# The recurrent mixer's gate and output projections as seven-product 2x2 block products

## The chip, the cores and the metric

One core of a Trainium2 chip. The metric is the device time of one launch in microseconds, and fewer is better. The engines have the profile's names: PE is TensorE (PEld its weight loads), DVE VectorE, ACT ScalarE, POOL GpSimd, SP SyncE. Every engine works through its own queue in order.

## The reference

Two encoder layers over 768 tokens (a sequence of 512 and one of 256) with 1024 channels. A layer adds half a SwiGLU FFN, a mixer, and half another FFN to x, each behind an RMS norm. The mixer of layer 0 is a bidirectional gated recurrence with eight heads of 128 channels; that of layer 1 is windowed attention. The change is in layer 0's mixer, which is, with the recurrence itself left out:

```
q, i, g, f_fw, f_bw = split(x @ w_in, 5)
o = scan_forward(q, k_f, i, f) + scan_backward(q, k_b, i, f)
o = o * rsqrt(mean(o * o, per head) + eps) * g_norm
return (o * silu(g)) @ w_o
```

Everything is float32.

## The kernel before, in words

A float32 product is made of three matmuls: each operand is split into a high part that the array takes exactly (a cast on ScalarE) and the rest (a subtraction on VectorE), and high x high, high x low and low x high are added up in PSUM. So each operand, weights too, costs one ScalarE and one VectorE pass (`split`, `plain_steps`).

Tokens are six blocks of 128 (`NBLK`), in two halves of three (`HB`); channels are eight blocks of 128. A plain projection `proj_tok` of 512 output columns takes, for each of six blocks, 8 x 3 matmuls of 128x512. The gate is two of them, `g0` and `g1`, and so is the output (`hg_o`), with 288 matmuls for the gate and 288 for the output.

A seven-product 2x2 block product cuts tokens, inner channels and output columns in halves, and forms seven products of half size in place of eight: `p1` to `p7` of sums and differences of the four weight quarters (`tok_steps`) with the four quarters of the input and their mixes `t1` to `t4` (`mix`, `FACTOR`). Each product has 3 blocks x 4 inner channel blocks x 3 matmuls = 36, all together 252. The value projection v already is one (`tok_quad`); the results are combined by adds from PSUM into its output tiles (`x11` to `x22`).

The mixer runs so: the v product, then eight scans (`hgrn_scan`), one per head, woven with the projections of later heads (`weave`, `hgrn_chunk`). A scan has seven levels; each level's scores (six 128x128 products in float32) need the queries and keys that the level before has scaled on VectorE. Into the last scan `g0` is woven in place of projections, and its result is evacuated by a Silu on ScalarE (L995) and multiplied by scan output and rstd on VectorE (L1001, 48 of 128x128). The gated blocks are then turned (transposes, L1019), scaled by the norm's gain and split (L1022, L1023), and multiplied with `w_o`. The results are added to x (L570), which has been reloaded from where it was spilled, and the next FFN's norm follows block by block (`after_block`).

Weights are loaded on SP's queue into buffers `wr`, split into buffers `w`, ahead of their use as far as free buffers allow (`ahead`, `load_next`, `done`). Which instruction stands where in an engine's queue is decided when the kernel is built: a tile layer puts the recorded instructions in order by its own estimates, except where the kernel pins them.

## Time and profile before

| what | value |
|---|---|
| median of three runs | 2788.37 us (2788.32 to 2788.64) |
| profiled execution | 2788.47 us |
| its span | 2786.7 us |
| TensorE busy | 2762.9 us, 99% |
| VectorE busy | 2191.5 us, 79% |
| ScalarE busy | 1343.8 us, 48% |
| the v product | 542 to 599 us of the span |
| scans with later heads' projections | 599 to 887 us |
| last scan with g0 | 887 to 937 us |
| g1, then output product | 937 to 975 us, 975 to 1042 us |

The profile is one execution; its span leaves out 1.8 us of the time. In a group's row the number behind the bar is the busy time of all its instructions and the mean of one in ns, then the idle time of the engine ahead of them and who ended it. A matmul's own length is modelled and overlaps the next one's; the pace of a run of them is the group's busy time over its count. In a timeline row the first number is the start in us.

### The profile page before, as it was taken

The numbers are of one execution on the slowest core, as the hardware profiler recorded it, in microseconds if no ns is written. First come the engines' busy times: TensorE is split into PE (matmuls) and PEld (weight loads), VectorE is DVE, ScalarE is ACT, GpSimd is POOL, SyncE is SP. The second block draws the span as 40 slices with busy tenths as digits, with TensorE's granted clock in tenths as the row PEclk, the third lists the DMA queues.
The fourth block names the chain that finished last, engine by engine and source line by source line (L and its number), as shares of the span: only waits on it lengthen the run. The fifth ranks groups of instructions, "written<-read, shape, count | busy, mean of one in ns | idle before, by whom it ended". The sixth has DMA issues, their size and how long they took to land.

```text
span 2786.7 us, 40646 instructions
## 1 busy us (share of the span) xinstructions
PE 2762.9 (99%) x15189; PEld 2569.4 (92%) x15189; DVE 2191.5 (79%) x3803; ACT 1343.8 (48%) x2479; POOL 376.8 (14%) x409
## 2 busy tenths in 40 slices
PE   8999999999999999999999999999999999999998
PEld 8999999989999889999999999999988889999998
DVE  8788788777887658878878887887848878778877
ACT  7344444634444435444444643444458855444443
POOL 2111111100000001211111121111002311211110
PEclk9999999999999999999999999999999999999999
DMA  6554554421111223555444365545422122655543
GB/s 176 125 131 114 123 144 128 145 69 39 39 39 31 81 81 81 144 134 124 121 114 121 84 144 127 131 114 122 129 72 76 40 66 74 148 133 129 117 114 107
DMA packets 331750, 294.53 MB, mean 106 GB/s; under 512 B 11848, under 2 KB 258080, under 8 KB 331552
## 3 DMA queue, kind: packets, MB, share of 16 engines
q1 hardware_dynamic: 294560, 213.42, 25.7%
q0 software_dynamic: 32688, 65.03, 13.9%
q10 hardware_dynamic: 4304, 13.49, 1.3%
q8 instruction: 119, 1.95, 0.3%
q14 instruction: 79, 0.65, 0.1%
HBM read 217.44 MB, written 9.44 MB: 81 GB/s over the span
## 4 chain that ended last, share of the span: by engine, by line
PE 96%; DVE 2%; ACT 1%; DMA 0%; issue 0%; DVEq 0%; ACTq 0%
PE ps L486 42%; PE ps L550 21%; PE ps L310 8%; PE ps L309 8%; PE ps L311 8%; PE ps L796 3%; PE ps L729 2%; PE ps L900 1%; PE ps L1291 1%; PE ps L876 1%; PE ps L380 1%; PE ps L1303 0%; PE ps L1253 0%; PE ps L1254 0%; PE ps L1304 0%; PE ps L1054 0%
## 5 line engine op out<-in xcount | busy, mean ns | idle before, releaser
L486 PE MATMUL ps<-big,w 128*128 128x384 f32 x6720 | 1169.3, 334 | 0.0
L486 PEld LDWEIGHTS ps<-big,w 128*128 128x128 f32 x6720 | 1165.9, 188 | 1.7 <-ACT tA L503 0.2
L205 ACT CAST w<-wr 128x512 fp32r<-128x512 f32 x600 | 416.9, 707 | 680.1 <-PE ps L486 277.7
L550 PE MATMUL ps<-w,big 128*128 128x512 f32 x2520 | 575.3, 389 | 0.0
L550 PEld LDWEIGHTS ps<-w,big 128*128 128x128 f32 x2520 | 472.8, 188 | 97.4
L206 DVE TENSOR_TENSOR w<-wr,w 128x512 fp32r<-128x512 f32 (+1 forms) x520 | 429.3, 830 | 159.4 <-ACT w L205 138.9
L572 DVE SCALAR_TENSOR_TENSOR x<-ps,x 128x512 f32<-128x512 f32 x468 | 302.5, 687 | 10.0 <-PE ps L311 9.9
L144 POOL DMA_DIRECT2D s<-wr x122 | 106.7, 877 | 1483.3 <-DMA wr<-in_ffn_w_dram 650.0
L309 PE MATMUL ps<-big,w 128*128 128x384 f32 x640 | 219.5, 345 | 1.1 <-ACT w L172 1.0
L310 PE MATMUL ps<-big,w 128*128 128x384 f32 x640 | 215.6, 337 | 0.6 <-DVE big L315 0.5
L311 PE MATMUL ps<-big,w 128*128 128x384 f32 x640 | 214.6, 335 | 0.0
L309 PE MATMUL ps<-w,big 128*128 128x512 f32 x528 | 210.9, 399 | 0.3 <-DVE big L1314 0.2
L311 PE MATMUL ps<-w,big 128*128 128x512 f32 x528 | 207.0, 392 | 0.5 <-DVE big L395 0.5
L310 PE MATMUL ps<-w,big 128*128 128x512 f32 x528 | 206.4, 391 | 0.0
L314 ACT CAST big<-tA 128x384 fp32r<-128x384 f32 x296 | 148.0, 513 | 113.8 <-DVE tA L518 36.2
L315 DVE TENSOR_TENSOR big<-tA,big 128x384 fp32r<-128x384 f32 x296 | 165.5, 570 | 6.7 <-ACT big L314 4.5
L206 POOL TENSOR_TENSOR w<-wr,w 128x512 fp32r<-128x512 f32 x80 | 133.3, 1666 | 185.8 <-ACT w L205 185.6
L144 POOL DMA_DIRECT2D wr<-wr x101 | 88.6, 877 | 422.0 <-DVE w L206 159.4
L172 ACT CAST w<-wr 128x1024 fp32r<-128x1024 f32 x84 | 88.2, 1052 | 107.3 <-PE ps L310 78.0
L173 DVE TENSOR_TENSOR w<-wr,w 128x1024 fp32r<-128x1024 f32 x84 | 102.1, 1223 | 41.7 <-ACT w L172 36.7
L212 DVE TENSOR_TENSOR wr<-wr,wr 128x512 f32<-128x512 f32 (+1 forms) x120 | 127.4, 1061 | 6.0 <-issue 5.7
L310 PEld LDWEIGHTS ps<-big,w 128*128 128x128 f32 x640 | 120.5, 188 | 1.9 <-DVE big L315 1.7
(198 smaller groups left out, 3390.8 us busy)
## 6 DMA issues: line engine op xcount, KB each, us to landing
wr<-in_ffn_w_dram SPq DMA_DIRECT2D x264, 512.0 KB, 3.9
s<-wr POOLq DMA_DIRECT2D x122, 256.0 KB, 4.8
s<-in_ffn_w_dram SPq DMA_DIRECT2D x120, 256.0 KB, 3.2
wr<-wr POOLq DMA_DIRECT2D x80, 256.0 KB, 3.9
wr<-in_hg_w_in_dram SPq DMA_DIRECT2D x36, 512.0 KB, 3.7
wr<-wr POOLq DMA_DIRECT2D x21, 512.0 KB, 4.6
spill<-x ACTq DMA_DIRECT2D x12, 512.0 KB, 4.0
x<-spill ACTq DMA_DIRECT2D x12, 512.0 KB, 3.2
```

The lines of the kernel that those rows point to most:

```text
L144: self.nc.gpsimd.dma_start(out, src, accum_op=ALU.add)
L205: nc.scalar.copy(h, src)
L206: (eng or nc.vector).tensor_sub(l, src, h.bitcast(F32))
L212: add = {"second": lambda: nc.vector.tensor_add(a11, a11, a21), "fourth": lambda: nc.vector.tensor_add(a12, a12, a11)}
L309: nc.tensor.matmul(out, a[0], b[0], start=first, stop=False)
L310: nc.tensor.matmul(out, a[0], b[1], start=False, stop=False)
L311: nc.tensor.matmul(out, a[1], b[0], start=False, stop=last)
L314: self.nc.scalar.copy(hi, src)
L315: self.nc.vector.tensor_sub(lo, src, hi.bitcast(F32))
L486: self.nc.tensor.matmul(ps, a[x], b[y], start=first and k == 0 and i == 0, stop=k == 3 and i == 2, skip_group_check=True,)
L550: nc.tensor.matmul(ps, a[x], w[y], start=name == chain and kp == 0 and q == 0, stop=kp == 1 and q == 2, skip_group_check=True,)
L572: self.nc.vector.scalar_tensor_tensor(x, ps, c, x, ALU.mult, ALU.add)
```

## The change

The gate and the output projection become seven-product block products through the same `tok_quad`, which now takes the order of products, the banks that they share (`chains`), the operands, an evacuation and a seed.

- **Operands of the gate.** They are the mixes t1 to t4 of the mixer's input, whose buffers are needed in between: `spill_factors` stores the eight tiles of 768 KB to DRAM from GpSimd's queue at the start of v, and `reload_factor` loads them on SP's, two at a time, when an earlier product of the gate has ended.
- **Last scan.** The gate's first products are woven into it, in half blocks of six matmuls. The rstd factor moves from VectorE's L1001 to ScalarE (`scaled`, 48 pieces of 128x128, 42 of them within the last scan, six at its end).
- **End of the gate.** `evac_g` adds the products up on VectorE, takes the Silu on ScalarE, and `gated` multiplies by scan output on VectorE (12 of 128x512). `turned` transposes four heads of half of the blocks at a time and evacuates them on ScalarE.
- **Output product.** `put` splits the turned tiles, `mixed` forms t1 to t4 from them on VectorE (`mix` with `early`: t3 and t2 first). The order `OUT` puts p2, p6 and p5 onto p1's banks and p7 and p4 onto p3's. Ahead of p6, p4 and p5 a ScalarE copy writes a value into the bank (`seed_o`, nine of 128x512) and the matmuls add to it.
- **Weights.** Both weight matrices are fetched in quarters, whose sums are made by accumulating DMAs on GpSimd's queue and by VectorE adds.
- x is reloaded in two halves; the masks move to another pool's buffers, the squares into spare room of kT and S.

```diff
+TCHAIN = {"p2": "p1", "p4": "p5", "p3": "p7"}
+OUT = ("p1", "p2", "p3", "p7", "p6", "p4", "p5")
...
-        sums = {"p6": (a11, a21), "p3": (a12, a11)}
+        second, fourth = (a11, a21), (a12, a11)
+        sums = {"p6": (second,), "p3": (fourth,)} if order == TOK else {}
+        behind = {"p2": (second, fourth)} if order == OUT else {}
...
+            for total, part in behind.get(name, ()):
+                for t, u in zip(total[kp], part[kp]):
+                    self.tc.keep_in_program_order(nc.vector.tensor_add(t, t, u))
...
+        inuse = lambda e: e[0] if len(e[1]) > 4 or e[0] < 4 else 0
+        while self.queue and sum(inuse(e) for e in self.loaded) + len(self.queue[0][1]) <= RAWBUFS:
...
+        if early:
+            put("t3", b22)
+            sub(b11, b11, b22)
+            put("t2", b11)
+            sub(b21, b21, b11)
+            put("t4", b21)
+            put("t1", b12)
+            return
...
+    def spill_factors(self):
+        self.kept = {}
+        for name in ("t3", "t2", "t1", "t4"):
+            for kp in range(2):
+                t = self.kept[(name, kp)] = self.dp.tile([P, 4 * H], F32, name=self.name("kept"))
+                self.nc.gpsimd.dma_start(t, self.ops[(name, kp)].bitcast(F32).rearrange("p a b c -> p (a b c)"))
+
+    def reload_factor(self, name):
+        for kp in range(2):
+            t = self.ops[(name, kp)] = self.big([P, 2, 2, H], F32R)
+            self.nc.sync.dma_start(t.bitcast(F32).rearrange("p a b c -> p (a b c)"), self.kept[(name, kp)])
...
+    def tok_quad(self, key, order, chains, ops, evac, seed=None):
+        nc = self.nc
+        banks, used = {}, []
+        for name in order:
             ws = [self.take((*key, name, kp)) for kp in range(2)]
-            chain = {"p2": "p1", "p4": "p5", "p3": "p7"}.get(name, name)
+            chain = chains.get(name, name)
             for i in range(HB):
+                fresh = (chain, i) not in banks
+                if fresh:
                     banks[(chain, i)] = self.ps()
                 ps = banks[(chain, i)]
+                if seed:
+                    seed(name, i, ps)
...
+                    if k == 1:
+                        if used and i:
+                            self.done(used.pop(0))
+                        yield name, i, 0
+                evac(name, i, ps)
+                if i == HB - 1:
+                    used += [(*key, name, kp) for kp in range(2)]
+                if i == HB - 1 or (used and not i):
+                    self.done(used.pop(0))
+                yield name, i, 1
+        for k in used:
+            self.done(k)
...
+        quad(("g",), w_in[:, 2 * D : 3 * D], TOK)
+        quad(("o",), w_o, OUT)
...
+        self.spill_factors()
+        for at in self.tok_quad(("v",), TOK, TCHAIN, self.ops, evac_v):
+            if at == ("p6", HB - 1, 1):
...
+        def evac_g(name, i, ps):
+            if name == "p1":
+                if i == 0:
+                    gq["x22"] = wide()
+                nc.scalar.activation(gq["x22"][:, i], ps, AF.Copy, scale=-1.0)
+                return
+            if name == "p2":
+                if i == 0:
+                    gq["x11"] = wide()
+                nc.scalar.activation(gq["x11"][:, i], ps, AF.Silu)
+                return
+            x22 = gq["x22"][:, i]
+            if name == "p5":
+                nc.vector.tensor_sub(x22, x22, ps)
+                if i == 0:
+                    gq["s22"] = wide()
+                nc.scalar.activation(gq["s22"][:, i], x22, AF.Silu)
+                gated(1, 1, i)
+            elif name in ("p4", "p3"):
+                q = "x21" if name == "p4" else "x12"
+                if i == 0:
+                    gq[q] = wide()
+                t = gq[q][:, i]
+                if name == "p4":
+                    nc.vector.tensor_add(t, ps, x22)
+                else:
+                    nc.vector.tensor_sub(t, ps, x22)
+                nc.scalar.activation(t, t, AF.Silu)
+                gated(int(name == "p3"), int(name == "p4"), i)
+            else:
+                nc.vector.tensor_add(x22, ps, x22)
+
+        def gated(half, part, i):
+            b = half * HB + i
+            sg = gq["s22" if half and part else f"x{part + 1}{half + 1}"][:, i]
+            u = vs[b][:, part * 512 : (part + 1) * 512]
+            nc.vector.tensor_mul(u, u, sg)
+
+        def scaled(first, last):
+            for b in range(NBLK):
+                for h in range(first, last):
+                    u = vs[b][:, h * P : (h + 1) * P]
+                    nc.scalar.activation(u, u, AF.Copy, scale=rs[:, h, b : b + 1])
+
+        uops, un = {}, {}
+
+        def turned(half, part):
+            t = un[(part, half)] = self.big([P, 2, 2, H])
+            for j in range(4):
+                h = 4 * part + j
+                pt = self.ps(H)
+                for i in range(HB):
+                    src = vs[half * HB + i][:, h * P : (h + 1) * P]
+                    nc.tensor.transpose(pt[:, i * P : (i + 1) * P], src, self.ident)
+                gn = self.cols[:, gn_row + h : gn_row + h + 1]
+                nc.scalar.activation(t[:, j // 2, j % 2, :], pt, AF.Copy, scale=gn)
+            if (part, half) != (0, 1):
+                for kp in range(2):
+                    self.put(f"b{part}{half}", kp, t[:, kp], uops)
+
+        def mixed(kp):
+            tiles = (un[(i // 2, i % 2)][:, kp] for i in range(4))
+            self.mix(*tiles, lambda name, src: self.put(name, kp, src, uops), True)
+
+        def gate():
+            need = {"p1": "t3", "p2": "t2", "p7": "t1", "p6": "t4"}
+            for at in self.tok_quad(("g",), TOK, TCHAIN, self.ops, evac_g):
+                if at[1:] == (HB - 1, 1) and at[0] in need:
+                    self.reload_factor(need[at[0]])
+                yield at
+
+        feed = itertools.chain(stream(), gate())
...
-        g0 = self.proj_tok("g0", put_g(0))
-        for _ in range(lead):
-            next(g0)
-        self.weave(scan(heads[-1]), g0, 24 - lead)
-        self.drain(g0)
-        rstds(1)
-        self.drain(self.proj_tok("g1", put_g(1)))
-        self.reload_x()
-        self.drain(self.out_proj("hg_o", 0, uT, None))
-        self.drain(self.out_proj("hg_o", 1, uT, next_row))
+            self.weave(scan(heads[h]), feed, 16 if h == 0 else 18)
+        rstds(0, HEADS - 1)
+        self.weave(scan(heads[-1]), feed, 20, also=lambda i: i < HEADS - 1 and scaled(i, i + 1))
+        rstds(HEADS - 1, HEADS)
+        scaled(HEADS - 1, HEADS)
+        for i in range(HB):
+            gated(0, 0, i)
+        for at in feed:
+            if at == ("p5", 1, 0):
+                turned(0, 0)
+            elif at == ("p4", 1, 1):
+                turned(1, 1)
+            elif at == ("p3", 1, 0):
+                turned(0, 1)
+                self.reload_x(range(HB))
+        def seed_o(name, i, ps):
+            src = {"p6": "first", "p4": "sum", "p5": "sum"}.get(name)
+            if src:
+                nc.scalar.activation(ps, oq[src][:, i], AF.Copy, scale=-1.0 if name == "p5" else 1.0)
+
+        def evac_o(name, i, ps):
+            if name == "p1":
+                if i == 0:
+                    oq["first"] = wide()
+                nc.scalar.activation(oq["first"][:, i], ps, AF.Copy, scale=-1.0)
+            elif name == "p3":
+                if i == 0:
+                    oq["third"], oq["sum"] = wide(), wide()
+                nc.scalar.copy(oq["third"][:, i], ps)
+            elif name == "p7":
+                nc.vector.tensor_sub(oq["sum"][:, i], ps, oq["third"][:, i])
+                nc.vector.tensor_add(xc(HB + i, 0), ps, xc(HB + i, 0))
+            elif name == "p6":
+                nc.vector.tensor_add(oq["sum"][:, i], ps, oq["sum"][:, i])
+            elif name == "p2":
+                nc.vector.tensor_add(xc(i, 0), ps, xc(i, 0))
+            elif name == "p4":
+                nc.vector.tensor_add(xc(i, 1), ps, xc(i, 1))
+                self.after_block(i, next_row)
+            else:
+                b = HB + i
+                nc.vector.tensor_sub(xc(b, 1), xc(b, 1), ps)
+                nc.vector.tensor_add(xc(b, 0), ps, xc(b, 0))
+                self.after_block(b, next_row)
+                if b >= 4:
+                    self.run_later()
+
+        chains = {"p2": "p1", "p6": "p1", "p5": "p1", "p7": "p3", "p4": "p3"}
+        for name, i, end in self.tok_quad(("o",), OUT, chains, uops, evac_o, seed_o):
+            if (name, i, end) == ("p1", 1, 0):
+                turned(1, 0)
+                self.reload_x(range(HB, NBLK))
+            elif (name, i, end) in (("p2", 0, 0), ("p2", 1, 1)):
+                mixed(int(i))
```

On each engine the rows ahead of the last scan and behind the mixer are the same as before, but for the eight stores.

PE, in the last scan, before: 12 of the gate's matmuls (L309, L310, L311) between two levels' scores (L796). These are the last ten of them and the scores.

```order
L311 MATMUL ps_1131_7994<-w_1112_7887,big_690_4709 128x512
L309 MATMUL ps_1131_7994<-w_1112_7887,big_690_4709 128x512
L310 MATMUL ps_1131_7994<-w_1113_7888,big_690_4709 128x512
L311 MATMUL ps_1131_7994<-w_1112_7887,big_690_4709 128x512
L309 MATMUL ps_1136_8041<-w_1056_7476,big_659_4611 128x512
L310 MATMUL ps_1136_8041<-w_1057_7477,big_659_4611 128x512
L311 MATMUL ps_1136_8041<-w_1056_7476,big_659_4611 128x512
L309 MATMUL ps_1136_8041<-w_1056_7476,big_659_4611 128x512
L310 MATMUL ps_1136_8041<-w_1057_7477,big_659_4611 128x512
L311 MATMUL ps_1136_8041<-w_1056_7476,big_659_4611 128x512
L796 MATMUL ps_1137_8049<-big_1119_7921,big_1124_7965 128x128 x4
L796 MATMUL ps_1138_8050<-big_1119_7921,big_1124_7965 128x128 x2
```

PE at the same place, now; L827 are the scores, L764 the gate's matmuls.

```order
L827 MATMUL ps_1142_8097<-big_1112_7892,big_1125_7990 128x128 x4
L827 MATMUL ps_1143_8098<-big_1112_7892,big_1125_7990 128x128 x2
L764 MATMUL ps_1132_8025<-w_1108_7871,big_690_4709 128x512 x2
L764 MATMUL ps_1132_8025<-w_1109_7872,big_690_4709 128x512
L764 MATMUL ps_1132_8025<-w_1108_7871,big_690_4709 128x512
L827 MATMUL ps_1148_8147<-big_1112_7892,big_1125_7990 128x128 x4
L827 MATMUL ps_1149_8148<-big_1112_7892,big_1125_7990 128x128 x2
L764 MATMUL ps_1150_8167<-w_1133_8039,big_1135_8045 128x512
L764 MATMUL ps_1150_8167<-w_1134_8040,big_1135_8045 128x512
L764 MATMUL ps_1150_8167<-w_1133_8039,big_1135_8045 128x512 x2
```

Between two levels' scores stand four matmuls of the gate where twelve stood.

ACT in the last scan, before: L826 copies the keys for a level's scores, L995 is the gate's Silu.

```order
L826 COPY big_1124_7965<-big_1120_7922 128x768 x2
L995 ACTIVATE tA_1134_8034<-ps_1131_7994 128x512
L826 COPY big_1124_7965<-big_1120_7922 128x768
L995 ACTIVATE tA_1139_8081<-ps_1136_8041 128x512
L826 COPY big_1124_7965<-big_1120_7922 128x768 x2
L995 ACTIVATE tA_1146_8143<-ps_1143_8103 128x512
L826 COPY big_1124_7965<-big_1120_7922 128x768
L995 ACTIVATE tA_1161_8237<-ps_1148_8150 128x512
```

ACT at the same place, now: L857 is the copy of the keys, L1078 the rescaling of scan output (x, by hrs), L323 the cast of a weight (w from wr).

```order
L323 CAST w_1144_8138<-wr_1044_7393 128x1024
L1078 ACTIVATE x_749_5109<-x_749_5109,hrs_5457 128x128
L1078 ACTIVATE x_742_5076<-x_742_5076,hrs_5457 128x128
L1078 ACTIVATE x_745_5092<-x_745_5092,hrs_5457 128x128
L1078 ACTIVATE x_748_5108<-x_748_5108,hrs_5457 128x128
L1078 ACTIVATE x_743_5077<-x_743_5077,hrs_5457 128x128
L1078 ACTIVATE x_746_5093<-x_746_5093,hrs_5457 128x128
L1078 ACTIVATE x_749_5109<-x_749_5109,hrs_5457 128x128
L1078 ACTIVATE x_742_5076<-x_742_5076,hrs_5457 128x128
L1078 ACTIVATE x_745_5092<-x_745_5092,hrs_5457 128x128
L1078 ACTIVATE x_748_5108<-x_748_5108,hrs_5457 128x128
L857 COPY big_1125_7990<-big_1113_7893 128x768
```

Ten rescalings and a weight's cast have come ahead of the copy of the keys.

DVE in the output product, before: adds into x from PSUM (L570) and two weight splits (L173).

```order
L570 TENSOR_TENSOR x_1232_8634<-ps_1242_8690,x_1232_8634 128x512
L570 TENSOR_TENSOR x_1233_8636<-ps_1243_8704,x_1233_8636 128x512
L570 TENSOR_TENSOR x_1234_8638<-ps_1244_8718,x_1234_8638 128x512
L173 TENSOR_TENSOR w_1247_8740<-wr_1218_8585,w_1246_8739 128x1024
L570 TENSOR_TENSOR x_1235_8640<-ps_1245_8732,x_1235_8640 128x512
L173 TENSOR_TENSOR w_1250_8753<-wr_1221_8597,w_1249_8752 128x1024
L570 TENSOR_TENSOR x_1230_8630<-ps_1252_8758,x_1230_8630 128x512
```

DVE in the output product, now: the mix of the turned blocks (L426, L427, L430, L432), the splits of the mixes (L324, 128x2x384) and of weights (L324, w), and the adds into x (L1147).

```order
L426 TENSOR_TENSOR big_1215_8577<-big_1244_8746,big_1215_8577 128x768
L324 TENSOR_TENSOR w_1254_8795<-wr_1171_8314,w_1253_8794 128x1024
L324 TENSOR_TENSOR big_1255_8806<-big_1215_8577,big_1255_8806 128x2x384
L430 TENSOR_TENSOR big_1202_8481<-big_1202_8481,big_1215_8577 128x768
L324 TENSOR_TENSOR w_1260_8828<-tA_1172_8316,w_1259_8827 128x512
L432 TENSOR_TENSOR big_1227_8651<-big_1227_8651,big_1202_8481 128x768
L324 TENSOR_TENSOR big_1256_8810<-big_1202_8481,big_1256_8810 128x2x384
L324 TENSOR_TENSOR w_1260_8828<-tA_1173_8317,w_1259_8827 128x512
L324 TENSOR_TENSOR big_1257_8814<-big_1227_8651,big_1257_8814 128x2x384
L324 TENSOR_TENSOR big_1258_8817<-big_1244_8746,big_1258_8817 128x2x384
L1147 TENSOR_TENSOR x_1235_8680<-ps_1243_8739,x_1235_8680 128x512
L427 TENSOR_TENSOR big_1244_8746<-big_1202_8481,big_1244_8746 128x768
```

A block of sixteen passes of 128x768, eight for each half of the inner channels, has come between the adds into x.

156 lines of the change are left out of this document (57 added, 99 removed).

## The prediction

> **What bounds the kernel now.** I read the page first: busy shares and the chain that ended last.
>
> ```profile
> span 2786.7 us, 40646 instructions
> PE 2762.9 (99%) x15189; PEld 2569.4 (92%) x15189; DVE 2191.5 (79%) x3803; ACT 1343.8 (48%) x2479; POOL 376.8 (14%) x409
> PE 96%; DVE 2%; ACT 1%; DMA 0%; issue 0%; DVEq 0%; ACTq 0%
> ```
>
> TensorE is never short of work, and the chain runs through it. So a matmul that goes is worth its whole pace, and an idle gap on TensorE costs its whole length. The profiled run took 2788.47 us, 1.8 more than its span, and 0.1 more than the median. Next the stages, in windows: the value projection v, the scans, the last scan with gate half g0, gate half g1, the output product, and the start of the FFN.
>
> ```profile
> core 0: us, PE busy (x) PEld busy (x) DVE busy (x) ACT busy (x) POOL busy (x), PEclk, DMA share, GB/s
> 542.00:599.30 57.30, 57.30 (x255) 47.45 (x255) 37.35 (x51) 23.37 (x34) 1.97 (x1) 1.00 0.26 74
> 599.30:887.00 287.70, 287.15 (x2007) 283.90 (x2006) 232.17 (x404) 127.07 (x230) 0.00 (x0) 1.00 0.14 41
> 887.00:937.50 50.50, 50.50 (x306) 44.52 (x305) 40.42 (x84) 22.70 (x40) 0.00 (x0) 1.00 0.11 34
> 937.50:975.00 37.50, 37.50 (x180) 31.34 (x179) 15.99 (x37) 14.28 (x21) 0.00 (x0) 1.00 0.31 103
> 975.00:1042.00 67.00, 66.91 (x314) 55.76 (x313) 33.66 (x52) 21.02 (x34) 1.73 (x2) 1.00 0.29 83
> 1042.00:1100.00 58.00, 58.00 (x343) 57.66 (x342) 48.94 (x69) 37.72 (x66) 10.12 (x7) 1.00 0.38 91
> ```
>
> TensorE has no gap in any of them. VectorE is busy for 80% beside the scans but for 43% and 50% in the g1 and output stages. The change fills just these two. The table of waits agrees: from 484 to 1100 us TensorE's matmuls waited twice.
>
> ```profile
> PE ps L796 <- ACT big L826: 0.5, 1, 0.5
> PE ps L310 <- DVE big L315: 0.3, 1, 0.3
> ```
>
> **What goes.** Gate and output lose 36 of 288 matmuls each: 72 of 128x512. The seven-product matmul is in the trace already, for v:
>
> ```profile
> L729 PE MATMUL ps<-w,big 128*128 128x512 f32 x252 | 57.3, 389 | 0.0
> ```
>
> 57.3/252 = 0.2274 us each (389 ns is the modelled length; they overlap), so 72 are worth **16.4 us**. The 48 transposes remain. All TensorE rows before the last scan and after the mixer are the same, so everything else is decided between 887 and 1042.
>
> **What comes: the last scan.** One level of the scan is a loop: scores on TensorE, two masked copies and the scaling of q on VectorE, the copy of k on ScalarE, scores. Its timeline:
>
> ```profile
> 916.25 1.50 PE L796 MATMUL ps<-big,big 128*128 128x128 f32 x12
> 917.34 1.07 DVE L815 COPY_PREDICATED big<-big,ps 128x512 f32<-128x512 uint8 x2 [0.48 <-PE ps L796]
> 917.83 0.84 ACT L826 COPY big<-big 128x768 f32<-128x768 f32 x1 [2.14 <-PE ps L796]
> 918.30 0.95 DVE L848 TENSOR_TENSOR big<-big,big 128x768 f32<-128x768 f32 x1
> 919.57 1.03 DVE L852 TENSOR_TENSOR big<-big,big 128x384 f32<-128x384 f32 x2
> 920.32 1.50 PE L796 MATMUL ps<-big,big 128*128 128x128 f32 x12
> ```
>
> Next scores can follow 916.25 no sooner than 919.25 (end of the q scaling), about 3.2 us with the hand-over. Between the two scores lie 12 product matmuls, so the scores themselves take 4.07 - 12 x 0.2274 = 1.34 us, and some 8 matmuls must lie between. In the new order one pair of levels has 4: 3.2 - 1.34 - 0.91 = 0.95 us of gap. At the next level there are 12 again (4.07 us), but the chain has a weight split of 1.22 (row below) ahead of the k scaling (1.03), then the k copy (0.84) among ten rescalings on ScalarE: 1.1 to the first masked copy, + 1.07 + 0.95 + 1.22 + 1.03 + 0.84 = 6.2, a gap of 2.1. The rescaling (48 head-by-block pieces, 42 of them in this scan) is priced by the nearest ScalarE row, a 128x128 copy, 8.8/42 = 0.21 each back to back; it replaces 48 VectorE pieces of 0.29:
>
> ```profile
> L906 ACT COPY x<-ps 128x128 f32<-128x128 f32 x42 | 8.8, 302 | 0.0
> L1001 DVE SCALAR_TENSOR_TENSOR tA<-x,hrs,tA 128x128 f32<-128x128 f32 x48 | 13.9, 348 | 20.2 <-ACT tA L995 20.2
> ```
>
> 42 x 0.21 = 8.8 us onto 22.7 of ScalarE work; with split casts and evacuations it has about 40 of 50 us. The other four hand-overs, an estimate from the same rows, cost 0.2 to 0.9 each, 1.75 together. Sum **4.8 us**, between 2.5 (only the counted gaps shrunk by work done early) and 8 (each rescaling 0.30).
>
> **The end of the gate.** Behind the last scan ScalarE switches function tables twice:
>
> ```profile
> 936.88 0.49 ACT L906 COPY x<-ps 128x128 f32<-128x128 f32 x2
> 937.39 1.28 ACT L984 ACT_TABLE_LOAD   x1
> 938.69 0.32 ACT L984 ACTIVATE hrs<-hss,eps 128x24 f32<-128x24 f32 x1
> 942.33 1.28 ACT L995 ACT_TABLE_LOAD   x1
> 943.62 0.60 ACT L995 ACTIVATE tA<-ps 128x512 f32<-128x512 f32 x1
> ```
>
> ```profile
> L907 DVE TENSOR_REDUCE hss<-tA 128x4 f32<-128x512 f32 x2 | 1.4, 678 | 0.0
> ```
>
> Now the first four evacuations of turned blocks queue behind both loads, the square root, six rescalings, a Silu and six copies of scan output: 2.6 + 0.3 + 1.3 + 0.6 + 1.3 + 1.0 (two squares, the second of half the width), and 1.3 of waiting for VectorE's two reductions and the reciprocal, 8.4 us. TensorE has 28 matmuls and 9 transposes (12 take 1.23 us from 1039.08 to 1040.31, quoted below), 7.3 us, until the next transpose needs the bank that the first evacuation (0.6) frees: a gap of 1.7. The two later rounds of transposes add, as an estimate, 1.4. Sum **3.1 us**, from 1.5 to 5. In the rows a load costs 1.28 and nothing more: 937.39 follows 937.37, and 938.69 follows at once. [...]
>
> **The output product.** Its operands are now made on VectorE: 8 subtractions and 8 splits of 128x768 in one block, beside weight splits and sums and three adds into x.
>
> ```profile
> L315 DVE TENSOR_TENSOR big<-big,big 128x768 fp32r<-128x768 f32 x16 | 14.6, 956 | 3.1 <-ACT big L314 3.1
> L173 DVE TENSOR_TENSOR w<-wr,w 128x1024 fp32r<-128x1024 f32 x38 | 46.3, 1223 | 22.1 <-ACT w L172 22.0
> L570 DVE TENSOR_TENSOR x<-ps,x 128x512 f32<-128x512 f32 x24 | 16.6, 690 | 26.3 <-PE ps L311 26.3
> ```
>
> From the second product's weight split until p7's weights are split VectorE has 16 x 0.91 (14.6/16) + 4 x 1.22 + 13 x 0.69 = 28.5 us, in order. TensorE has p1, p2, p3 and 12 transposes for cover, 108 x 0.2274 + 1.2 = 25.8. So p7 waits at least 2.7; the mix itself cannot start before the last turned blocks are evacuated, and p3's second split is late by about 0.8. Sum **4.1 us**, from 2.6 to 6.2. The nine seeds cost nothing: a product of the same bank ended at least a product (8.2 us) earlier, and two blocks (5.4 us) cover the last sum (0.69) and the seed (0.6, from a ScalarE 128x512 like the Silu above); without that cover 1.3 for each of the two later products.
>
> **The seam to the FFN.**
>
> ```profile
> 1039.08 1.47 PE L380 MATMUL ps<-ident_r,big 128*128 128x128 f32 x12
> 1040.31 0.60 PE L309 MATMUL ps<-big,w 128*128 128x384 f32 x2
> 1041.11 0.19 PEld L310 LDWEIGHTS ps<-big,w 128*128 128x128 f32 x1 [0.40 <-DVE big L315]
> ```
>
> Before, only a 0.4 us gap. Now the last product needs two adds per block instead of one (0.69 more) ahead of the norm, and evacuations stand behind the norms of two blocks. **1.8 us**, from 0.7 to 2.6.
>
> **Transfers.** Eight 768 KB stores in v, from GpSimd's queue ahead of the mask cast, and eight loads on SP's, one product ahead:
>
> ```profile
> POOL big L128 <- DVE w L315: 34.7, 1, 34.7
> wr<-in_hg_w_o_dram SPq DMA_DIRECT2D x8, 512.0 KB, 5.4
> x<-spill ACTq DMA_DIRECT2D x6, 512.0 KB, 3.2
> ```
>
> GpSimd idled 34.7 us before that cast, and 6.3 MB in 57.3 us add 110 GB/s to 74. A load scaled by size lands in 4.8 to 8.1 us, less than a product of 36 matmuls (8.2). The last load (t4) is queued behind output weights whose buffers VectorE frees late; I take 0, at most 4 us. The x loads in two halves are as early as before.
>
> **Sum.** 2788.5 - 16.4 + 4.8 + 3.1 + 4.1 + 1.8 = 2785.9 for a profiled run; against the median 0.1 less, **2785.8**. The lower ends give 7.3 us of gaps (2779), the upper 21.8 (2794): the forecast's own range.
>
> **Rivals.** First, the gaps close: the gaps were counted one by one, but a gap at one hand-over gives VectorE and ScalarE time that the next has to spare. The v stage speaks for it, a seven-product form with no gap at 65% VectorE. Against it, VectorE's 28.5 us against 25.8 do not go away. With about 4 us left, 2776 (2772 to 2782).
>
> Second, slower: VectorE becomes the bound from the gate's p5 to the output's p7. The p5 to p3 rows hold 24 x 0.69 + 3 x 1.22 + 6 x 0.91 = 25.7, so 54.2 us with the above, against 53.9 on TensorE (216 x 0.2274 + 48 x 0.10). Any idleness of VectorE then lengthens the stretch; the forecast's 7.2 us of gap there make its share 89%. Its busiest windows show 232.17/287.70 = 81% and 48.94/58 = 84%. At 81% the stretch takes 66.9 us, 13.0 of gap, 19.6 with scan and seam: 2791.6. At 75% 18.4 and 25.0: **2797** (2794 to 2802, the latter at 70%). It is slower by over 5.6 us from a share under 78%. For it: every split waits for a cast on a ScalarE that is itself full. Against it: in those windows VectorE mostly waited for TensorE, without need.
>
> Third, the t4 load is late by its full 4 us: 2790.
>
> **Chances.** Forecast 0.42, of which 0.12 lies below 2782.8; gaps close 0.29; VectorE bound 0.25; late load 0.04. A measurement tells 0.2% (5.6 us) from no change. Faster by more 0.12 + 0.29 = 0.41; within 0.30 + 0.04 = 0.34; slower 0.25. The range leaves out the lowest third of the closing gaps and the upper two fifths of the VectorE bound: 2774 to 2798.
>
> **What would show it.** The output stage's VectorE share over 85% until p7, with a gap of about 3 us ahead of p7's first matmul; gaps of 1 and 2 us between scan levels; gaps at the gate's last transposes ended by ScalarE; none ended by a DMA. Four gap groups under 1 us each would prove the first rival. I am wrong if gaps lie outside 887 to 1042, in v for instance, or if matmuls slow down under the added transfers.

## The result, and the profile after

The changed kernel takes 2783.04 us (median of 15 runs, 2781.01 to 2785.44) against 2788.39 us (15 runs, 2788.01 to 2788.88) in the same session: 5.3 us less, a ratio of 0.9981 with an interval of 0.9974 to 0.9988. The forecast was 2785.8, a gain of 2.6: the gain is about twice that. Besides the median the scatter has changed: 4.4 us between the ends of its runs, where the kernel before has 0.9.

The head of the page of the changed kernel; the profiled run took 2783.55 us:

```profile
span 2781.6 us, 40766 instructions
PE 2750.1 (99%) x15117; PEld 2555.3 (92%) x15117; DVE 2228.3 (80%) x3825; ACT 1387.6 (50%) x2586; POOL 393.9 (14%) x431
```

The 72 matmuls are gone from TensorE's count (15189 to 15117). The FFN starts at 1034.72 us where it started at 1040.31, and v at 542.4 instead of 541.99, so the mixer behind v's start is 6.0 us shorter. 16.4 us of matmuls went, and with them the 0.5 us wait of the kernel before, which stood in the last scan but one (0.6 counted as below); so 11.0 us came back. The table of waits from 484 to 1100 us says where (line, wait in total, times, longest):

```profile
PE ps L764 <- ACT big L1140: 2.6, 2, 2.3
PE ps L827 <- ACT big L857: 1.9, 1, 1.9
PE ps L319 <- DVE big L324: 0.7, 2, 0.4
PE ps L827 <- DVE big L879: 0.7, 1, 0.7
PE ps L764 <- DVE w L324: 0.6, 1, 0.6
PE ps L932 <- DVE big L919: 0.4, 1, 0.4
PE ps L908 <- ACT big L901: 0.2, 1, 0.2
PE ps L318 <- ACT big L323: 0.2, 1, 0.2
```

No wait is ended by a DMA, and none by a seed (L1130). L827 is the scan's scores, L764 the seven-product matmul, L318 and L319 the FFN's first. The stages in windows, now the last scan, the end of the gate, the output product until p7, its rest, with v ahead:

```profile
core 0: us, PE busy (x) PEld busy (x) DVE busy (x) ACT busy (x) POOL busy (x), PEclk, DMA share, GB/s
542.00:599.30 57.30, 57.30 (x255) 47.51 (x254) 37.49 (x51) 23.46 (x34) 4.42 (x6) 1.00 0.51 165
884.00:935.00 51.00, 47.70 (x287) 41.20 (x286) 41.42 (x77) 36.47 (x87) 2.62 (x3) 1.00 0.44 145
935.00:970.00 35.00, 35.00 (x186) 29.33 (x185) 27.76 (x40) 28.27 (x54) 3.51 (x4) 1.00 0.69 186
970.00:1000.00 30.00, 26.76 (x119) 21.23 (x118) 28.05 (x36) 19.70 (x34) 0.00 (x0) 0.98 0.37 124
1000.00:1037.00 37.00, 36.38 (x170) 30.05 (x169) 28.00 (x45) 23.04 (x40) 2.02 (x2) 0.97 0.35 91
```

v carries twice the traffic (165 GB/s, before 74) at no cost to TensorE: 57.30 of 57.30. The gaps are in the last scan (3.3 us idle) and in the output product until p7 (3.2), where VectorE is busy for 28.05 of 30 us. The clock column is new: 0.98 and 0.97, where the kernel before has 1.00 in every stage from 542 to 1100 us. In finer windows around p7:

```profile
995.00:998.00 3.00, 1.21 (x4) 0.67 (x4) 3.00 (x5) 3.00 (x6) 0.00 (x0) 1.00 0.21 59
998.00:1000.00 2.00, 1.82 (x5) 1.50 (x6) 1.94 (x4) 2.00 (x5) 0.00 (x0) 0.68 0.30 83
1000.00:1002.00 2.00, 2.00 (x6) 1.56 (x5) 0.83 (x2) 0.60 (x2) 0.00 (x0) 0.50 0.38 107
1002.00:1004.00 2.00, 2.00 (x9) 1.59 (x9) 2.00 (x4) 0.00 (x0) 0.00 (x0) 0.96 0.84 250
```

About 2 us after the gap has ended TensorE runs at half its clock for 3.4 us: 2 x 0.32 + 2 x 0.50 + 2 x 0.04 = 1.7 us lost. The table of waits cannot show this; TensorE counts as busy.

Each gap is also a little longer than its wait says. A matmul's end is modelled at 389 ns while the next starts 227 ns after it, so the wait counts 0.16 us too little. By starts, the two counted gaps of the scan, rows of the timeline:

```profile
906.06 1.17 PE L764 MATMUL ps<-w,big 128*128 128x512 f32 x4
907.94 1.58 PE L827 MATMUL ps<-big,big 128*128 128x128 f32 x12 [0.71 <-DVE big L879]
909.28 2.99 PE L764 MATMUL ps<-w,big 128*128 128x512 f32 x12
914.22 1.60 PE L827 MATMUL ps<-big,big 128*128 128x128 f32 x12 [1.95 <-ACT big L857]
```

907.94 - 906.06 - 4 x 0.2274 = 0.97 us, and 914.22 - 909.28 - 12 x 0.2274 = 2.21. The gap ahead of p7, between p3's last matmuls and p7's first:

```profile
988.17 6.19 PE L764 MATMUL ps<-w,big 128*128 128x512 f32 x26 [0.63 <-DVE w L324]
996.66 1.21 PE L764 MATMUL ps<-w,big 128*128 128x512 f32 x4 [2.30 <-ACT big L1140]
```

996.66 - 988.17 - 26 x 0.2274 = 2.58 us. The copy of p3 that this wait names (L1140) stands behind casts that waited for VectorE's mix (L430):

```profile
993.09 0.84 ACT L323 CAST big<-big 128x768 fp32r<-128x768 f32 x1 [1.94 <-DVE big L430]
996.03 0.58 ACT L1140 COPY big<-ps 128x512 f32<-128x512 f32 x1
```

### The profile page after: what moved, and what is told of

It is laid out like the page before. It is cut to its first block, busy times and chain, and to the rows that moved or that the text cites. A ratio compares the mean times of both kernels' runs of the same rounds, so it can differ in the third digit from the quotient of the medians.

```text
span 2781.6 us, 40766 instructions
## 1 busy us (share of the span) xinstructions
PE 2750.1 (99%) x15117; PEld 2555.3 (92%) x15117; DVE 2228.3 (80%) x3825; ACT 1387.6 (50%) x2586; POOL 393.9 (14%) x431
## 3 DMA queue, kind: packets, MB, share of 16 engines
q8 instruction: 119, 1.95, 0.3%
## 4 chain that ended last, share of the span: by engine, by line
PE 95%; DVE 2%; ACT 2%; DMA 0%; issue 0%; DVEq 0%; ACTq 0%
PE ps L517 42%; PE ps L581 21%; PE ps L319 6%; PE ps L318 6%; PE ps L320 6%; PE ps L764 5%; PE ps L827 3%; PE ps L932 1%; PE ps L1418 1%; PE ps L908 1%; PE ps L389 1%; PE ps L1430 0%; PE ps L1380 0%; PE ps L1381 0%; PE ps L1431 0%; PE ps L1181 0%
## 5 line engine op out<-in xcount | busy, mean ns | idle before, releaser
L581 PE MATMUL ps<-w,big 128*128 128x512 f32 x2520 | 575.6, 389 | 0.0
L581 PEld LDWEIGHTS ps<-w,big 128*128 128x128 f32 x2520 | 472.6, 188 | 97.9 <-DVE x L603 0.3
L318 PE MATMUL ps<-big,w 128*128 128x384 f32 x640 | 219.3, 345 | 2.0 <-ACT w L175 1.0
L319 PE MATMUL ps<-big,w 128*128 128x384 f32 x640 | 215.5, 337 | 0.9 <-DVE big L324 0.9
L323 ACT CAST big<-tA 128x384 fp32r<-128x384 f32 x296 | 148.0, 513 | 114.3 <-DVE tA L549 36.4
L764 PE MATMUL ps<-w,big 128*128 128x512 f32 x756 | 179.7, 395 | 3.2 <-ACT big L1140 2.6
L764 PEld LDWEIGHTS ps<-w,big 128*128 128x128 f32 x756 | 141.4, 189 | 33.5 <-ACT big L1140 3.5
L324 DVE TENSOR_TENSOR big<-tA,big 128x384 fp32r<-128x384 f32 x296 | 166.2, 572 | 6.6 <-ACT big L323 4.5
L318 PE MATMUL ps<-w,big 128*128 128x512 f32 x336 | 134.7, 401 | 0.3 <-DVE big L1441 0.2
L215 DVE TENSOR_TENSOR wr<-wr,wr 128x512 f32<-128x512 f32 (+1 forms) x120 | 122.9, 1024 | 14.2 <-issue 10.2
L320 PE MATMUL ps<-w,big 128*128 128x512 f32 x336 | 132.2, 393 | 0.5 <-DVE big L404 0.5
L319 PE MATMUL ps<-w,big 128*128 128x512 f32 x336 | 131.6, 392 | 0.0
L318 PEld LDWEIGHTS ps<-big,w 128*128 128x128 f32 x640 | 119.9, 188 | 3.2 <-ACT w L175 1.3
```

What stands on the lines that cost most here:

```text
L318: nc.tensor.matmul(out, a[0], b[0], start=first, stop=False)
L319: nc.tensor.matmul(out, a[0], b[1], start=False, stop=False)
L320: nc.tensor.matmul(out, a[1], b[0], start=False, stop=last)
L323: self.nc.scalar.copy(hi, src)
L324: self.nc.vector.tensor_sub(lo, src, hi.bitcast(F32))
L581: nc.tensor.matmul(ps, a[x], w[y], start=name == chain and kp == 0 and q == 0, stop=kp == 1 and q == 2, skip_group_check=True,)
```

## The experiments

Twelve kernels ran, each beside the kernel before on its chip (2788.4 to 2788.7 there).

| kernel | median us (range, runs) | ratio to before, interval |
|---|---|---|
| changed kernel again | 2783.02 (2781.45 to 2784.81, 11) | 0.9981 [0.9972, 0.9990] |
| gate alone changed | 2786.09 (2784.83 to 2787.23, 11) | 0.9992 [0.9983, 1.0000] |
| gap ahead of p7 filled | 2781.65 (2780.38 to 2783.15, 10) | 0.9975 [0.9966, 0.9985] |
| both large gaps filled | 2782.94 (2782.65 to 2783.40, 11) | 0.9980 [0.9971, 0.9989] |
| late splits on GpSimd | 2786.70 (2784.47 to 2788.57, 11) | 0.9994 [0.9985, 1.0003] |
| late mix | 2778.90 (2777.71 to 2779.41, 5) | 0.9965 [0.9952, 0.9977] |
| early rescaling | 2781.27 (2779.81 to 2781.84, 7) | 0.9973 [0.9963, 0.9984] |
| late mix, early rescaling | **2775.31** (2774.60 to 2776.59, 5) | 0.9953 [0.9939, 0.9967] |
| 22 pieces woven | 2782.37 (2780.66 to 2783.34, 11) | 0.9976 [0.9967, 0.9985] |
| before, gap of 1.0 us | 2790.52 (2790.30 to 2790.95, 10) | 1.0007 [0.9998, 1.0016] |
| before, gap of 2.95 us | 2793.59 (2792.67 to 2794.43, 10) | 1.0018 [1.0009, 1.0027] |
| before, gap of 5.55 us | 2797.43 (2796.75 to 2797.94, 5) | 1.0032 [1.0019, 1.0044] |

**The changed kernel again.** No edit; a second profile of the same program.

> The changed kernel once more, for a second profile and for the comparison on the same chip. If the scatter of its times (4.4 us in 15 runs, 0.9 before) comes from spells in which the granted clock halves after a gap on TensorE, each spell of 3.4 us costs 1.7 us: the times should differ by multiples of about 1.7 us, the slower ones with the lower mean clock, and this profile should show as many spells as its time lies above 2781. If the scatter comes from transfers, the clock is the same in all and gaps are ended by DMAs. Median 2783.0, range 2781 to 2786.

The median repeats. This profile (2784.48 us) has two half-clock spells, the one at p7 and one behind the scan's 2 us gap, which the first profile (2783.55 us) lacks:

```profile
912.00:914.00 2.00, 0.04 (x2) 0.02 (x1) 2.00 (x6) 2.00 (x7) 0.00 (x0) 1.00 0.00 0
914.00:916.00 2.00, 2.00 (x10) 2.00 (x11) 2.00 (x5) 2.00 (x6) 0.00 (x0) 0.53 0.00 0
916.00:918.00 2.00, 2.00 (x9) 1.72 (x9) 2.00 (x5) 1.61 (x6) 0.00 (x0) 0.62 0.00 0
```

2 x 0.47 + 2 x 0.38 = 1.7 us again. So the same gap brings a spell in one run and none in another: a source of scatter. The times do not stand in steps of 1.7 us, as was expected, and with one spell more this profile is only 0.9 us slower than the first; so the spells are not the whole scatter.

**Gate alone changed.** The output projection stays as before (turned blocks written as split halves by ScalarE and VectorE, two plain halves behind them).

```diff
-        quad(("o",), w_o, OUT)
+        self.plan_out("hg_o", w_o)
...
-                nc.scalar.activation(t[:, j // 2, j % 2, :], pt, AF.Copy, scale=gn)
...
+                nc.scalar.activation(hi, pt, AF.Copy, scale=gn)
+                nc.vector.scalar_tensor_tensor(lo, pt, gn, hi.bitcast(F32), ALU.mult, ALU.subtract)
...
+        self.drain(self.out_proj("hg_o", 0, uT, None))
+        self.drain(self.out_proj("hg_o", 1, uT, next_row))
```

> Only the gate is a seven-product block product; the output projection is the plain one of 288 matmuls with its operands split as before. Theory: the gate alone takes 36 matmuls away (8.2 us) and brings the last scan's gaps (3.3 us by the waits, about 4 with the pipeline's refill) and in some runs a half-clock spell there (1.7 us): 2783 to 2785.5, so that the output's half brings little or nothing (8.2 less 4 of gaps, 1.7 of spell and the seam). Rival: the gate pays for all, the output stage loses as much as it saves or more: 2781 to 2783. Second rival: both halves gain alike: 2785.5 to 2786.

2786.09 us: above the range of the first theory and 0.1 above that of the second rival, by which both halves gain alike. The gate's half brings 2.3 us of its 8.2, the output's half 3.05. The scan's waits are the same 1.9 + 0.7 + 0.4 + 0.2, and its profile has a spell at 914 to 918.

**Gap ahead of p7 filled.** Fifteen matmuls whose result nothing reads, on operands that are ready, keep TensorE at work in the gap (`NFILL` is 15).

```diff
+            if name == "p7":
+                idle = self.ps()
+                h = uops[("b11", 1)][:, 1, 0, :]
+                for j in range(NFILL):
+                    self.tc.keep_in_program_order(
+                        nc.tensor.matmul(idle[:, :H], h[:, :P], h, start=j == 0, stop=j == NFILL - 1)
+                    )
```

> Fifteen matmuls of 128x384 into a bank that nobody reads (2.6 us) stand ahead of the output's p7, where TensorE waited 2.6 us. Theory: the wait ahead of p7 ends when it ended, so the work costs nothing, but TensorE is never idle long enough for its clock to fall: the half-clock spell behind p7's wait is gone, median 2781.3 (1.7 us less than the changed kernel), and the scatter shrinks. Rival: the clock falls for another reason (added transfers, or the mere count of small gaps): the spell stays, and the time is the same or up to 2.6 us longer.

1.4 us less than the changed kernel, though TensorE does more. The clock at p7 is 1.00 throughout:

```profile
995.00:998.00 3.00, 3.00 (x18) 2.92 (x17) 3.00 (x4) 2.87 (x6) 0.00 (x0) 1.00 0.00 0
```

What follows is no earlier for it: the next wait for a copy of p3, 0.3 us around 998 us, is there as in the first profile of the changed kernel. So the spell went with the idle time and not with the lateness, and the median is 1.4 us lower. The gap in the scan still brings one (from 914.81 us).

**Both large gaps filled.** The same, and 20 small matmuls of the identity in the scan's 2 us gap.

```diff
+            if h == HEADS - 1 and l == 4:
+                for _ in range(20):
+                    self.tc.keep_in_program_order(
+                        nc.tensor.matmul(pss[0][:, :P], self.identr, self.identr, start=True, stop=True)
+                    )
```

> The changed kernel with unread matmuls in both of its long gaps: 15 of 128x384 ahead of p7, as before, and 20 of 128x128 ahead of the last scan's fifth level of scores, where TensorE waited 1.9 us. Theory: both waits end when they ended, no half-clock spell is left between 880 and 1040 us, and the scatter that was left with one gap filled (2.8 us) goes with it: median 2780.5, lowest to highest under 1.5 us. Rival: the spell in the last scan comes from elsewhere and stays: 2781.5, with the scatter.

Half came true. No spell is left between 880 and 1040 us, and the runs lie within 0.75 us of each other instead of 3.4 to 4.4, as the theory says. The median did not fall below the kernel with one gap filled: it is 1.3 us above it. Behind the inserted work another wait has come up, which neither profile of the changed kernel has:

```profile
PE ps L830 <- DVE big L887: 2.0, 2, 1.3
```

**Late splits on GpSimd.** The low parts of t4 and t1 are taken from VectorE's block ahead of p7.

```diff
+        (eng or self.nc.vector).tensor_sub(lo, src, hi.bitcast(F32))
...
-            self.mix(*tiles, lambda name, src: self.put(name, kp, src, uops), True)
+            late = lambda name: nc.gpsimd if name in ("t4", "t1") else None
+            self.mix(*tiles, lambda name, src: self.put(name, kp, src, uops, late(name)), True)
```

> In the output's mix the low parts of t4 and t1 (four of 128x768) are subtracted on GpSimd in place of VectorE; their products come two later than p7. Theory: VectorE's block of 28 us ahead of p7 is what p7 waits for; 3.6 us less of it takes the 2.6 us gap to under 0.5 and with it the half-clock spell: 2778 to 2780. Rival: p7 waits for ScalarE, which is slowed by its own queue and not by VectorE: the gap stays above 2 us, 2782 to 2784. Second rival: GpSimd and VectorE hinder each other, VectorE's 128x768 passes take longer than 0.95 us beside it, and little is won.

3.7 us slower than the changed kernel; the second rival is borne out. The timeline at p7, GpSimd and the VectorE rows beside it:

```profile
987.44 4.74 POOL L420 TENSOR_TENSOR big<-big,big 128x768 fp32r<-128x768 f32 x2 [22.25 <-ACT big L419]
988.47 2.01 DVE L429 TENSOR_TENSOR big<-big,big 128x768 f32<-128x768 f32 x1
990.40 2.59 DVE L420 TENSOR_TENSOR big<-big,big 128x768 fp32r<-128x768 f32 x1
996.27 4.46 POOL L420 TENSOR_TENSOR big<-big,big 128x768 fp32r<-128x768 f32 x2 [4.10 <-ACT big L419]
998.96 2.92 DVE L324 TENSOR_TENSOR w<-big,w 128x512 fp32r<-128x512 f32 x2
```

A subtraction takes GpSimd 2.3 us, and VectorE's passes of 0.95 take 2.0 and 2.6 meanwhile, a pair of splits 2.92 instead of 1.28. The passes that stand clear of GpSimd's rows, at 986.40 and 992.92 us, take 0.95 as before, so in this run VectorE is held up beside GpSimd; by what, the rows do not show. p7 waits 3.3 us for the copies instead of 2.6 and 1.8 for weight splits instead of 0.6; in a window around the spell behind it the clock loses 10 x 0.34 = 3.4 us instead of 1.7:

```profile
998.00:1008.00 10.00, 8.88 (x26) 6.23 (x25) 7.77 (x9) 3.41 (x6) 2.73 (x2) 0.66 0.28 80
```

0.7 + 1.2 + 1.7 make 3.6 of the 3.7.

**Late mix.** The last subtraction and the splits of t4 and t1, which no product needs before p4 (t4) and p5 (t1), are recorded behind p7's start, so that p7's weight splits stand ahead of them in VectorE's queue.

```diff
-            sub(b21, b21, b11)
-            put("t4", b21)
-            put("t1", b12)
-            return
+            def rest():
+                sub(b21, b21, b11)
+                put("t4", b21)
+                put("t1", b12)
+            return rest
...
+            elif (name, i, end) in (("p7", 0, 0), ("p7", 1, 1)):
+                rest.pop(0)()
```

> The part of the output's mix that p4 and p5 need (one subtraction and the splits of t4 and t1, for both halves of the inner channels: six VectorE passes of 128x768, 5.5 us) is recorded behind the start of p7 in place of ahead of it. Theory: VectorE's 28 us ahead of p7's weights become 23, less than TensorE's 25.8; the gap ahead of p7 (2.6 us) and the half-clock spell behind it (1.7 us) go: 2778.5 to 2780. Rival: VectorE is only late later; the gap comes back ahead of p4 or at the seam to the FFN: 2782 to 2784.

4.1 us less than the changed kernel. No wait at p7 is left, the clock stays at 1.00, and VectorE works without a pause through the place, as it does in the 12 us behind it:

```profile
985.00:998.00 13.00, 13.00 (x59) 10.76 (x58) 13.00 (x18) 9.34 (x16) 0.00 (x0) 1.00 0.28 83
```

So p7's gap was VectorE's order, although the wait named ScalarE's copy. The gap in the scan and a spell behind it (from 914.52 us) are still there.

**Early rescaling.** The 36 rescalings of the first six heads are done one scan earlier.

```diff
+            if h == HEADS - 2:
+                rstds(0, h)
+                also = lambda i: i < HEADS - 2 and scaled(i, i + 1)
...
-        self.weave(scan(heads[-1]), feed, 20, also=lambda i: i < HEADS - 1 and scaled(i, i + 1))
+        rstds(HEADS - 2, HEADS - 1)
+        self.weave(scan(heads[-1]), feed, 20, also=lambda i: i == 0 and scaled(HEADS - 2, HEADS - 1))
```

> 36 of the 48 rescalings move one scan earlier, where ScalarE is 44% busy; of the last scan's 42 six remain, and one more function table switch comes. The order around the last scan's levels shifts with it: 16 matmuls in place of 4 between two levels. Theory: the rescalings and the order that they force make the last scan's gaps (0.7, 1.9, 0.4, 0.2 us by the table of waits): these fall under 1 us together, 2780.5. Rival: the gaps come from VectorE's weight splits and sums, which stay: gaps of 2 us or more remain, 2782.5 to 2784; or the earlier scan shows gaps of its own.

1.75 us less. In the last scan 0.5 + 0.3 + 0.4 + 0.2 of wait remain, of 3.3; p7's 2.3 and its spell stay. The scan before it takes the 36 pieces without a gap. The order shifted too, though: 16 matmuls stand where the changed kernel has 4 between two levels, so that this run alone does not tell the two apart.

**22 pieces woven.** The same gaps attacked by the order instead: each level gets its share of 22 pieces of gate work in place of 20, so that no pair of levels has only 4 matmuls between. The first block of p5 is then gated before the last head's output is written, so that head's part of the block goes ungated; the work is the same.

```diff
-        self.weave(scan(heads[-1]), feed, 20, also=lambda i: i < HEADS - 1 and scaled(i, i + 1))
+        self.weave(scan(heads[-1]), feed, 22, also=lambda i: i < HEADS - 1 and scaled(i, i + 1))
```

> The changed kernel with one number changed: 22 in place of 20 pieces of the gate are spread over the last scan. All 42 rescalings stay in it, but the matmuls between its levels are now 13, 28, 8, 18, 12, 18, 18 in place of 13, 26, 4, 12, 21, 9, 18. It tells apart what the early rescalings brought (1.75 us). If the order alone did it: the gap at the 4 (0.7) goes, that at the next level (1.9) falls to under 1, 2781.3 to 2782. If ScalarE's rescalings themselves hold up the levels: gaps of 2 us or more remain, 2782.5 to 2784.

Only 0.65 us less than the changed kernel, inside the scatter, and between the ranges of the two theories. The 0.7 at the pair with 4 matmuls is gone, but the wait for the k copy is not:

```profile
PE ps L827 <- ACT big L857: 2.1, 2, 1.3
```

More work between the levels does not remove the wait where the copy stands behind rescalings on ScalarE; taking those away left 0.5.

**Late mix and early rescaling together.**

> Both the late mix and the 36 rescalings one scan earlier. If the two losses are separate, their gains add up: 1.75 for the rescalings and 3 to 4.5 for the mix, 2776.5 to 2778.5, with no half-clock spell between 880 and 1040 us and so a scatter under 1.5 us. If they share a cause (one spell, ended by either), it is no better than the better of the two.

2775.31 us, 13.1 less than the kernel before and 7.7 less than the changed one; the two alone brought 4.1 + 1.75 = 5.9. It is 1.2 us below the range expected. The rest fits the spells: the late mix alone still has one in its scan, and here the clock is 1.00 from 542 to 1030 us. The scatter did not come down as expected: 2.0 us in 5 runs, not under 1.5, with no spell in the mixer of the profile; what causes that part is not known. Its waits from 484 to 1100 us are all short:

```profile
PE ps L319 <- DVE big L324: 0.6, 2, 0.3
PE ps L830 <- ACT big L860: 0.5, 2, 0.3
PE ps L935 <- DVE big L922: 0.4, 1, 0.4
PE ps L830 <- DVE big L882: 0.3, 1, 0.3
PE ps L911 <- ACT big L904: 0.2, 1, 0.2
PE ps L318 <- ACT big L323: 0.2, 1, 0.2
```

2.2 us in 8 waits, and 0.16 uncounted in each: 3.5, against the 3.3 that this kernel lacks of the 16.4. The match is rough, since the kernel before has two waits of its own.

**A gap put into the kernel before.** There, between the two halves of the output product, four small matmuls feed one, four or eight ScalarE copies in a chain, and a transpose of the last lets the second half start.

```diff
...
+        for _ in range(NCOPY - 1):
+            nc.scalar.copy(t, t)
+        last = pin(nc.tensor.transpose(self.ps()[:, :P], t[:, :P], self.ident))
+        with self.tc.issue_after(last.ins):
+            self.drain(self.out_proj("hg_o", 1, uT, next_row))
```

> The kernel before, with a gap made on purpose between the halves of the output projection: four small transposes, one ScalarE copy of 128x512 that waits for them, and one transpose that waits for the copy, with the second half's matmuls behind it. The gap should be about 1.1 us (0.6 of copy and the hand-overs). Theory: a gap this short does not lower the clock, 2788.5 + 1.5 = 2790.0 with the transposes. Rival: any gap does, 2791.7.

> The same with four copies in a row, a gap of about 2.6 us, as long as that ahead of p7. Theory: a gap of this length lowers the clock in some or all runs, for 3.4 us at half: 2788.5 + 3.0, and 1.7 more with a spell, so 2791.5 to 2793.2, scattered by up to 1.7. Rival: the spells in the changed kernel need the several gaps near one another, and one alone does nothing: 2791.5 without scatter.

> The same with eight copies, a gap of about 4.7 us. Theory: longer than the spell's own 3.4 us, so every run has a spell: 2788.5 + 5.1 + 1.7 = 2795.3 with little scatter. Rival: no spell, 2793.6.

The 1.0 us gap has no spell: +1.84 us, clock 1.00 throughout. The gap of 2.95 us, from 1005.45 to 1008.4, in windows:

```profile
1006.00:1008.00 2.00, 0.00 (x0) 0.00 (x0) 1.55 (x2) 1.91 (x4) 0.00 (x0) 1.00 0.41 122
1008.00:1010.00 2.00, 1.60 (x6) 1.37 (x7) 0.00 (x0) 0.35 (x1) 0.00 (x0) 0.82 0.82 224
1010.00:1012.00 2.00, 2.00 (x6) 1.51 (x6) 0.00 (x0) 0.00 (x0) 0.00 (x0) 0.50 0.58 173
1012.00:1014.00 2.00, 2.00 (x9) 1.58 (x8) 0.69 (x1) 0.00 (x0) 0.00 (x0) 0.83 0.02 5
```

Half clock for 3.4 us, 1.7 lost by these rows. The gaps came out longer than expected (2.95 and 5.55 us, not 2.6 and 4.7), and both times lie above the figures given. From the gap's end to the FFN's first matmul the profiles take 35.43 us with the short gap, 37.05 with the middle and 37.41 with the long one: the spells cost 1.6 and 2.0 us there. By the medians the middle gap takes 3.07 us more than the short one, 1.1 above the 1.95 by which it is longer; the 0.5 between 1.6 and 1.1 stays open. With 5.55 us of gap the spell begins inside it:

```profile
1010.00:1012.00 2.00, 0.00 (x0) 0.00 (x0) 0.00 (x0) 1.90 (x4) 0.00 (x0) 0.50 0.69 200
1012.00:1014.00 2.00, 1.75 (x5) 1.46 (x6) 0.00 (x0) 0.20 (x1) 0.00 (x0) 0.50 0.33 99
```

6.8 us at half clock (1009.68 to 1016.51), 4.3 of them behind the gap: 2.1 us, and by the medians 6.91 - 4.55 = 2.4 above the gap.

## Why the prediction was right, and where it was not

The mechanism was the forecast's in the main: 72 matmuls of 0.2274 us go, and gaps give most of it back, above all at two of the four places named. A third gave nothing, and a loss that the forecast lacks came in. Point by point:

- **Matmuls, 16.4.** As counted. v is the same to 0.1 us, and behind the first 30 us no gap outside 884 to 1042 is new.
- **Last scan, 4.8.** The two counted gaps are 0.97 and 2.21 us (predicted 0.95 and 2.1), ended by the engines named. The four estimated ones (1.75) came as two, 0.4 and 0.2, with 0.16 more each: 4.1 in all. The rescaling was priced too low: 0.31 us a piece (15.0/48), not 0.21, where the upper bound had 0.30. ScalarE carried it (36.47 of 51 us); what it held up visibly is the copy of k, which starts at 913.33, right behind ten rescalings:

```profile
910.39 3.04 ACT L1078 ACTIVATE x<-x,hrs 128x128 f32<-128x128 f32 x10
```

- **End of the gate, 3.1.** Measured none. This is the term that was mis-sized most. ScalarE's chain began at 937.64, before the last product of the scan was done, and its one wait for VectorE in between, for the reciprocal, took 0.26 where 1.3 was put in. The rows around the hand-over:

```profile
937.64 0.60 ACT L936 ACTIVATE big<-ps 128x512 f32<-128x512 f32 x1 [1.32 <-PE ps L932]
939.54 1.28 ACT L1030 ACT_TABLE_LOAD   x1
943.28 1.28 ACT L1052 ACT_TABLE_LOAD   x1
945.11 1.98 ACT L1091 ACTIVATE big<-ps,cols 128x384 f32<-128x384 f32 x4
945.73 0.55 PE L1089 MATMUL ps<-ident_r,x 128*128 128x128 f32 x3
```

7.5 us to the first evacuation, not 8.4, and against TensorE's work this was just in time. The loads still cost 1.28, and the next row starts within 0.02 us.

- **Output product, 4.1.** 4.0 by starts: 2.58 ahead of p7's first matmuls (2.7 predicted), 0.6 at the next, 0.8 at the second split of p3. VectorE was busy for 28.05 of 30 us, above the 85% asked for, and the late mix took the gap away. Seeds: nine of 0.6 us, no TensorE wait.
- **Seam, 1.8.** By starts 0.4 ahead of the FFN's first matmul, where the kernel before had no gap, and 0.6 behind its first two, where that had 0.25: about 0.8 more. The norms and adds were mostly done in time.
- **Transfers, 0.** No wait is ended by a DMA. The reloads land in 8.1 us at the median, a product's length, but a product ahead of their use.
- **Not foreseen: the clock.** One spell of 1.7 us in the profile. Up to the FFN's first matmul the sum 4.1 + 4.0 + 0.4 + 1.7 = 10.2 stands beside the 11.0 that came back; 0.8 lies in differences too small to be named.

The four terms of the forecast, 13.8, measure 8.9: 4.9 too high, of which the spell and the unnamed rest, less the wait that went, took back about 2. So it is in part luck that the forecast lies within 2.8 us of the time: a term that it did not have made up for part of the two that were too high. The test that four gap groups under 1 us would prove the first rival failed, two being about 2; the late t4 load did not occur. The VectorE bound did not come in the changed kernel, but the version with GpSimd shows what it costs: there the same place holds 3.3 + 1.8 us of waits.

## What to carry to other kernels

In a kernel whose TensorE is 99% busy, matmuls removed are paid back wherever the loop between two engines was just covered by them (here with 4.1 + 4.0 + 0.4 = 8.5 us of gaps for 16.4 of matmuls); count the cover at each hand-over before and after, and move what is not needed yet behind the first thing that is (here worth 4.1 us by order alone). Where TensorE is what the rest waits for, look at the granted clock behind each gap: here the 2.58 us ahead of p7 were followed by a half-clock spell that lost 1.7 more; filling such a gap with work that nobody reads may pay (1.4 us at p7, nothing more in the scan). A rescaling or split that is "off the path" belongs in the stage whose engine has room (the rescalings one scan earlier: 1.75 us less), not on the engine that is named idle on average (splits on GpSimd, busy for 14%: 3.7 us more).

## What the hardware showed that was not expected

**Half-clock spells behind short gaps.** One core. In the mixer a 1.0 us gap brought no spell, gaps of 1.9 to 2 us brought one in some profiles and none in others, gaps of 2.3 to 3 us one of 3.4 us in each profile, and gaps of 3.3 us (late splits on GpSimd) and 5.55 us one of 6.8. Where it begins varies: 2 us after the gap ahead of p7 in one profile, 0.9 us after the gap of 2.95, at once behind the 2 us gap in the scan, and 0.4 us after the gap at p7 with early rescaling.

The clock records of the traces show a pattern. Apart from the one that runs past each kernel's end, every spell lasts 3.413 us or twice that, and the spells of one profile begin whole multiples of it apart: in the second profile of the changed kernel they begin at 914.11, 999.44 and 2183.87 us, 25 and 347 times 3.4133 apart. So cut each profile into windows of this length, with an edge at a spell's start, and add up the time in which TensorE is idle in each window. In the 14 profiles, without start and end, all 15 windows at full clock with 1.92 us or more of idle time were followed by a spell, six of the ten with 1.63 to 1.90, and none with 1.35 or less. In the profile of the kernel before one window is followed by a spell, with 1.73 us; in the first of the changed kernel two are, with 1.65 (ahead of the spell at p7) and 2.08, and the next in length there, with 1.14, is not. So in these profiles the spells go with the idle time within one window, not with the length of a gap: in the second profile the scan's gap (912.03 to 913.98) lies inside the window from 910.69, and a spell follows; in the first an edge at 913.41 cuts it into 1.14 and 0.81, and none does.

In layer 1 a spell cost no time. Every kernel, that before too, has a gap of about 1.9 us there (L1304 in the kernel before, until 2186.51), and in ten of the 14 profiles a spell follows it. The kernel before, behind that gap:

```profile
2188.00:2190.00 2.00, 1.70 (x9) 1.70 (x10) 2.00 (x5) 1.32 (x3) 0.00 (x0) 0.67 0.36 104
```

VectorE is busy for 2.00 of these 2.00 us, and from the gap's end to the end of the kernel it takes 600.1 to 600.3 us with a spell and without.

**VectorE beside GpSimd.** Beside two fp32 subtractions of 128x768 on GpSimd (4.74 us) two VectorE passes took 4.6 us, where two take 1.9 without: VectorE lost more than the 1.9 us that it was spared.
